# The experts of a mixture-of-experts layer: weight splits traced ahead as one stream, other operations placed behind them

## The chip, the core and the metric

The kernel runs on one core of a Trainium2 chip. The metric is the device time of one execution in microseconds (us). The engines named below are PE (TensorE, matrix products), ACT (ScalarE), DVE (VectorE), POOL (GpSimd) and SP (SyncE, which only issues transfers here).

## The reference, cut to what matters

The layer is a diffusion-transformer block: a gated linear attention and a Hyena convolution, mixed by a projection, then a mixture of experts by expert choice, then a final norm. The change touches only the experts. There are 16 of them; each picks 128 of the 1024 rows.

```
def _ec_moe(h, w_router, w_gate, w_up, w_down):
    cap = EC_FACTOR * L // N_EXPERTS                      # 2 * 1024 // 16 = 128
    aff = jax.nn.softmax((h @ w_router).astype(jnp.float32), axis=-1)
    vals, idx = lax.top_k(jnp.swapaxes(aff, 1, 2), cap)
    xs = h[bidx, idx]
    hid = jax.nn.silu(jnp.einsum('becd,edf->becf', xs, w_gate)) * jnp.einsum('becd,edf->becf', xs, w_up)
    y = jnp.einsum('becf,efd->becd', hid, w_down) * vals[..., None]
    return jnp.zeros_like(h).at[bidx, idx].add(y)
```

All three weight matrices of an expert are 1024x1024 in float32, so the experts read 16 x 3 x 4 MiB.

## The kernel before, in words

A product of float32 accuracy is made of three products: each operand is split into a rounded part `hi` and the remainder `lo`, and `mm3` (lines 150 to 152) adds hi*hi, hi*lo and lo*hi in PSUM. `split` makes the parts: ACT copies the source to `hi` (line 144), DVE subtracts `hi` from the source to get `lo` (line 147).

An expert has three units of products: `w_gate`, `w_up` and `w_down`, called here g, u and d with the expert's number (g3, u3, d3). A unit goes over k = 0 to 7, one weight tile of 128x1024 for each k ("tile k" below). `expert_mm` does it: the tile `raw` is loaded (`expert_tile`; `eraw` for gate and up, `erawl` for down; SP issues the load), split into `ehi` (5 buffers) and `elo` (4 buffers), and multiplied in six matmuls of 512 columns into `pex` (3 buffers in PSUM). So ACT can split a tile only when PE has finished the tile five before it, and DVE only when PE has finished the one four before it. The units come in the order g0, u0, g1, d0, u1, g2, d1, and so on to u15, d15: the gate of the next expert stands between up and down.

Around the units stands other work, each on the in-order queues of its engines:

- `transposed(e, xs, True)` turns the rows of an expert: 8 transposes on PE (`ptx`, line 1341), 8 scalings on ACT (`tt`, line 1346), then a split into `thi` and `tlo` in two halves. Even and odd experts use different `thi` and `tlo`. It is traced in the middle of u(e-1).
- `route(e)` finds an expert's rows: a comparison on DVE (`oh`, line 1320), 8 small matmuls (`pi`), three small DVE operations (`pv`, `ix`, `iv`), and a gather of the rows on POOL (`xs`, one buffer). It is traced in the middle of u(e-2).
- the silu of the gate on ACT (`sg`, line 1354), its product with up on DVE (`sg`, line 1375), and `transposed(e, sg)` of the result, traced in the middle of g(e+1).
- the scaled output `y` on DVE (line 1386), and its scatter-add into DRAM on POOL (`d_acc`, line 1387).

The order of the instructions of one engine is not written out: a scheduler lays them out from the order in which they are traced and from its own estimate of when each can start. `tc.issue_after(x)` keeps each operation of its block, on x's engine, behind x. Behind the experts, eight row tiles `xf` are read back, normed (a square on ACT, an rsqrt of small steps, a scaling on DVE at line 1414) and written, and the last expert's `y` is added to its own rows (lines 1417 to 1425).

Of the kernel before, what the change touches and what calls it, by code (L numbers as in the profile page):

```python
# [10 lines left out]
F32 = mybir.dt.float32  # L11
F32R = mybir.dt.float32r
BF16 = mybir.dt.bfloat16
I32 = mybir.dt.int32
AF = mybir.ActivationFunctionType
# [5 lines left out]
P = 128  # L21
D = 1024
# [4 lines left out]
KT = D // P  # L27
# [5 lines left out]
E = 16  # L33
# [65 lines left out]
def tile_gla_hyena_moe(ctx: ExitStack, tc: tile.TileContext, io: dict, out: bass.AP):  # L99
    nc = tc.nc  # L100
    V, A, T, G, SY = nc.vector, nc.scalar, nc.tensor, nc.gpsimd, nc.sync
# [26 lines left out]
    def pB(shape, name="pb"):  # L128
        return psum.tile(shape, F32, name=name, tag="pB", bufs=2)
# [12 lines left out]
    def split(hi, lo, src, act=True):  # L142
        if act:
            A.activation(hi, src, AF.Copy)  # L144
        else:
            V.tensor_copy(hi, src)
        V.tensor_sub(lo, src, hi.bitcast(F32))  # L147

    def mm3(out_, lh, ll, rh, rl, first, last):
        T.matmul(out_, lh, rh, start=first, stop=False)  # L150
        T.matmul(out_, lh, rl, start=False, stop=False)  # L151
        T.matmul(out_, ll, rh, start=False, stop=last)  # L152
# [40 lines left out]
    def cv(shape, dt=F32, name="cv"):  # L193
        return cp.tile(shape, dt, name=name, tag="cv", bufs=7)
# [24 lines left out]
    for o in range(2):  # L219
        raw = cv([P, 2, HYW], name="w3raw")  # L220
# [19 lines left out]
    for c in range(2):  # L240
        cs = slice(c * 512, (c + 1) * 512)
        ps = pB([P, 512], name="pmlp")
# [8 lines left out]
    for c in range(2):  # L251
        cs = slice(c * 512, (c + 1) * 512)
        ps = pB([P, 512], name="pmlp")
# [268 lines left out]
    ahead = []  # L522
# [393 lines left out]
    def mid_tile(name, dt=F32):  # L916
        return mid.tile([P, D], dt, name=name, tag="x", bufs=NX)
# [18 lines left out]
    state, qe, at = [None] * (2 * NT), [None] * NT, [None] * NT  # L936
# [85 lines left out]
    def row_of(i, pool, **kw):  # L1022
        t = pool.tile([P, D], F32, name=f"row{i}", **kw)
        bcast_row(t, d_mod[0, i * D:(i + 1) * D], D)
        return t
# [175 lines left out]
    pse = ctx.enter_context(tc.tile_pool(name="pse", bufs=1, space=PSUM, reuse_waits="tile"))  # L1201

    def mt(shape, dt, name, tag, bufs):
        return mp.tile(shape, dt, name=name, tag=tag, bufs=bufs)

    def pT(shape, name):
        return pse.tile(shape, F32, name=name, tag="t", bufs=2)

    NR, NL, NHI, NLO, NS, NXS = 14, 8, 5, 4, 4, 1
    used = [0]  # L1210
    KB, KU = 5, 2

    def expert_tile(w, e, k, queue=SY):
        if w == "w_down":
            raw = mt([P, D], F32, "erawl", "erawl", NL)
        else:
            used[0] += 1
            if (used[0] - 1) % (NR + NX) < NX:
                raw = mid_tile("eraw")
            else:  # L1220
                raw = rawr.tile([P, D], F32, name="eraw", tag="eraw", bufs=NR)
        queue.dma_start(raw, io[w][0, e, k * P:(k + 1) * P, :])
        return raw

    loaded = {(w, k): expert_tile(w, 0, k) for w in ("w_gate", "w_up", "w_down") for k in range(KT)}

    def expert_mm(w, e, xt, between=None, at=KB):
        ps = pse.tile([P, D], F32, name="pex", tag="ex", bufs=3)
        for k in range(KT):
            raw = loaded[w, k] if e == 0 else expert_tile(w, e, k)  # L1230
            hi = mt([P, D], F32R, "ehi", "ehi", NHI)
            lo = mt([P, D], F32R, "elo", "elo", NLO)
            split(hi, lo, raw)
            for h in range(2):
                hs = slice(h * 512, (h + 1) * 512)
                mm3(ps[:, hs], xt[0][:, k], xt[1][:, k], hi[:, hs], lo[:, hs], k == 0, k == KT - 1)
            if between and k == at:
                between()
        return ps

    pos = mp.tile([P, E, NT], BF16, name="pos")

# [74 lines left out]
    def route(e):  # L1317
        pi = pT([P, 5], "pi")
        oh = mt([P, NT, P], BF16, "oh", "s2", NS)
        V.tensor_tensor(oh, slot[:, None, :].to_broadcast([P, NT, P]),  # L1320
                        pos[:, e, :, None].to_broadcast([P, NT, P]), op=ALU.is_equal)
        for t in range(NT):
            T.matmul(pi, oh[:, t], tv[:, e, t], start=t == 0, stop=t == NT - 1)
        ix = tiny.tile([P, 1], I32, name="ix", bufs=4)
        pv = tiny.tile([P, 5], F32, name="pv", bufs=4)
        V.tensor_copy(pv, pi)
        last = V.tensor_add(ix, pv[:, 0:1], pv[:, 1:2])
        iv = tiny.tile([P, 1], F32, name="iv", bufs=4)
        V.tensor_reduce(iv, pv[:, 2:5], AX.X, ALU.add)
        xs_ = mt([P, D], F32, "xs", "xs", NXS)  # L1330
        gather = G.indirect_dma_start(out=xs_, out_offset=None, in_=d_h[:, :],
                             in_offset=bass.IndirectOffsetOnAxis(ap=ix[:, :1], axis=0))
        return iv, ix, xs_, last, gather

    def transposed(e, src, norm=False):
        hi = mt([P, KT, P], F32R, "thi", f"thi{e % 2}", 1)
        lo = mt([P, KT, P], F32R, "tlo", f"tlo{e % 2}", 1)
        for g in range(2):
            pt = pT([P, 4, P], "ptx")
            for k in range(4):  # L1340
                T.transpose(pt[:, k], src[:, (4 * g + k) * P:(4 * g + k + 1) * P], ident)  # L1341
            if norm:
                tt = mt([P, 4, P], F32, "tt", "s2", NS)
                for k in range(4):
                    kk_ = 4 * g + k
                    A.activation(tt[:, k], pt[:, k], AF.Identity, bias=fcol[:, 0, kk_:kk_ + 1], scale=gfcol[:, kk_:kk_ + 1])  # L1346
                pt = tt
            split(hi[:, 4 * g:4 * g + 4], lo[:, 4 * g:4 * g + 4], pt)
        return hi, lo

    def gate_part(e, xt, between=None):
        pg = expert_mm("w_gate", e, xt, between)
        sg = mt([P, D], F32, "sg", "sg", 1)
        A.activation(sg, pg, AF.Silu)
        return sg

    A.preload_act_table_set("silu_and_others")
    routed = [route(0)]
    xt = transposed(0, routed[0][2], True)
    routed.append(route(1))  # L1360
    select(NF, E - NF, "b", 2)
    with tc.issue_after(routed[0][3].ins):
        sg = gate_part(0, xt)
    m5 = row_of(5, mp)
    for e in range(E):
        ahead = []

        def next_rows():
            if e + 1 < E:
                ahead.append(transposed(e + 1, routed[e + 1][2], True))  # L1370
            if e + 2 < E:
                routed.append(route(e + 2))

        pu = expert_mm("w_up", e, xt, next_rows, KU)
        V.tensor_mul(sg, pu, sg)
        if e + 1 < E:
            sg_next = gate_part(e + 1, ahead[0], lambda: ahead.append(transposed(e, sg)))
        else:
            ahead = [None, transposed(e, sg)]
        xt_next, ht = ahead  # L1380
        py = expert_mm("w_down", e, ht)
        iv, ix = routed[e][0:2]
        if e + 1 == E:
            break
        y = mt([P, D], F32, "y", "y", 1)
        V.scalar_tensor_tensor(y, py, iv, m5, op0=ALU.mult, op1=ALU.mult)  # L1386
        G.indirect_dma_start(out=d_acc[:, :], out_offset=bass.IndirectOffsetOnAxis(ap=ix[:, :1], axis=0),  # L1387
                             in_=y, in_offset=None, compute_op=ALU.add)
        xt, sg = xt_next, sg_next


    tc.keep_in_program_order(A.preload_act_table_set("natural_log_exp_and_others"))
# [6 lines left out]
    for i in range(NT):  # L1399
        xt = rawr.tile([P, D], F32, name="xf", tag="eraw", bufs=NR)  # L1400
# [45 lines left out]
```

## Time and profile before

| what | value |
|---|---|
| runs | 1383.40, 1385.44, 1390.76 us; median 1385.44 |
| profiled execution, its own time | 1382.24 us |
| its span on the core | 1380.5 us |
| PE busy with matmuls | 1275.1 us (92%) |
| DVE busy | 1149.6 us (83%) |
| ACT busy | 806.4 us (58%) |
| experts' products, first to last start | 769.6 to 1354.3 us |

The span is the stretch in which the profiler saw the core at work; the 1.74 us between it and the execution's time lie around it. Busy times are sums of recorded durations. The record of a matmul reaches past the start of the next one, so a PE that is shown busy throughout can still lose time between two starts; starts are the safer measure.

### The profile page before, as it was taken

To read this page: it belongs to the slowest core of one execution; us is meant where nothing else is said; L and a number is where in the kernel's file an instruction comes from. 1 tells how busy PE (TensorE), PEld (TensorE's weight loads), DVE (VectorE), ACT (ScalarE), POOL (GpSimd) and SP (SyncE) were. 2 spreads that over 40 slices of the span, in tenths; PEclk is the share of its full clock that TensorE was granted. 3 is DMA by queue.
4 is the path that set the end of the run, shared out by engine and by line. 5 is a ranking of instruction groups with operands and counts; after the bars stand their busy time and mean duration, and the time that the engine had idled before them with its cause. 6 is when DMAs were issued, how large, how long until landed. Compare 5 with 4: busy or idle time off the path is not lost.

```text
span 1380.5 us, 21546 instructions
## 1 busy us (share of the span) xinstructions
PE 1275.1 (92%) x7720; PEld 1043.0 (76%) x7720; DVE 1149.6 (83%) x1920; ACT 806.4 (58%) x1228; POOL 130.1 (9%) x142
## 2 busy tenths in 40 slices
PE   6978999999999997987996899999999999999982
PEld 4777888687898896766775678888888888877762
DVE  6877838899778778878756799999999999988885
ACT  3247453211221415885553578888888888877864
POOL 1110000010100110000000000011111111012010
PEclk9998999999999998998996799999999999999996
DMA  7893541774655536766668689999999999999765
GB/s 223 315 241 118 177 128 47 229 218 146 187 169 167 154 100 186 176 158 174 221 230 348 241 316 357 358 394 381 395 381 390 385 389 383 372 366 370 265 204 223
DMA packets 154362, 354.81 MB, mean 257 GB/s; under 512 B 28389, under 2 KB 74013, under 8 KB 153999
## 3 DMA queue, kind: packets, MB, share of 16 engines
q1 hardware_dynamic: 134911, 292.84, 59.7%
q0 software_dynamic: 19344, 60.61, 15.7%
q8 instruction: 60, 0.98, 0.3%
q14 instruction: 47, 0.39, 0.1%
HBM read 310.89 MB, written 50.89 MB: 262 GB/s over the span
## 4 chain that ended last, share of the span: by engine, by line
PE 45%; DVE 4%; DMA 2%; issue 1%; ACT 1%; SPq 0%; POOLq 0%; POOL 0%; DVEq 0%; ACTq 0%
PE pex L151 13%; PE pex L152 12%; PE pex L150 12%; PE ptx L1341 2%; DVE elo L147 1%; PE psel L1252 1%; PE pout L150 1%; DMA eraw<-w_up 1%; PE pout L151 1%; DVE xf L1414 1%; PE pout L152 1%; DVE state L635 0%; PE po L1123 0%; PE po L1127 0%; DMA xs<-d_h,ix 0%
## 5 line engine op out<-in xcount | busy, mean ns | idle before, releaser
L147 DVE TENSOR_TENSOR elo<-eraw,ehi 128x1024 fp32r<-128x1024 f32 x256 | 302.5, 1219 | 13.0 <-issue 5.9
L151 PE MATMUL pex<-elo,thi 128*128 128x512 f32 x768 | 306.0, 398 | 4.7 <-DVE elo L147 4.4
L150 PE MATMUL pex<-ehi,thi 128*128 128x512 f32 x768 | 305.4, 398 | 2.3 <-ACT thi L144 1.3
L152 PE MATMUL pex<-ehi,tlo 128*128 128x512 f32 x768 | 303.4, 395 | 0.8 <-DVE tlo L147 0.8
L144 ACT ACTIVATE ehi<-eraw 128x1024 fp32r<-128x1024 f32 x256 | 265.0, 1068 | 50.2 <-PE pex L152 49.3
L151 PEld LDWEIGHTS pex<-elo,thi 128*128 128x128 f32 x768 | 145.2, 189 | 40.4 <-DVE elo L147 10.4
L150 PEld LDWEIGHTS pex<-ehi,thi 128*128 128x128 f32 x768 | 145.2, 189 | 34.1 <-ACT thi L144 1.7
L152 PEld LDWEIGHTS pex<-ehi,tlo 128*128 128x128 f32 x768 | 145.0, 189 | 31.7 <-DVE tlo L147 1.2
L147 DVE TENSOR_TENSOR elo<-erawl,ehi 128x1024 fp32r<-128x1024 f32 x128 | 149.4, 1218 | 6.4 <-ACT ehi L144 5.6
L144 ACT ACTIVATE ehi<-erawl 128x1024 fp32r<-128x1024 f32 x128 | 131.3, 1057 | 19.6 <-PE pex L152 18.0
L144 ACT ACTIVATE whi<-wraw 128x1024 fp32r<-128x1024 f32 x30 | 31.8, 1060 | 104.9 <-DMA wraw<-w_in 28.4
L542 PE MATMUL phy<-xh,whi 128*128 128x512 f32 x192 | 77.2, 402 | 11.3 <-ACT whi L144 11.3
L543 PE MATMUL phy<-xl,whi 128*128 128x512 f32 x192 | 76.0, 396 | 0.0
L150 PE MATMUL pvg<-whi,xh 128*128 128x256 f32 x256 | 73.2, 286 | 0.0
L151 PE MATMUL pvg<-wlo,xh 128*128 128x256 f32 x256 | 72.4, 283 | 0.0
L152 PE MATMUL pvg<-whi,xl 128*128 128x256 f32 x256 | 72.4, 283 | 0.0
L1387 POOL DMA_INDIRECT d_acc<-y,ix x15 | 34.6, 2308 | 392.5 <-DVE y L1386 392.5
L1346 ACT ACTIVATE tt<-ptx,fcol,gfcol 128x128 f32<-128x128 f32 x128 | 48.7, 463 | 33.9 <-PE ptx L1341 33.9
L545 PE MATMUL phy<-xh,wlo 128*128 128x512 f32 x192 | 61.9, 399 | 0.0
L438 ACT ACTIVATE D<-pdft 128x512 f32<-128x512 f32 x32 | 19.1, 597 | 68.9 <-PE pdft L468 39.4
L147 DVE TENSOR_TENSOR wlo<-wraw,whi 128x1024 fp32r<-128x1024 f32 x30 | 36.6, 1221 | 21.2 <-ACT whi L144 21.1
L467 PE MATMUL pdft<-kk,fmat 128*128 128x128 f32 x256 | 52.1, 286 | 0.3 <-ACT D L438 0.2
(452 smaller groups left out, 2596.3 us busy)
## 6 DMA issues: line engine op xcount, KB each, us to landing
eraw<-w_gate SPq DMA_DIRECT2D x128, 512.0 KB
eraw<-w_up SPq DMA_DIRECT2D x128, 512.0 KB
erawl<-w_down SPq DMA_DIRECT2D x128, 512.0 KB
wt<-w_ada SPq DMA_DIRECT2D x48, 512.0 KB
wraw<-w_in SPq DMA_DIRECT2D x30, 512.0 KB
kspec<-d_spec SPq DMA_DIRECT2D x16, 512.0 KB
xt<-x SPq DMA_DIRECT2D x8, 512.0 KB
d_spec<-ue POOLq DMA_DIRECT2D x8, 512.0 KB, 5.9
```

The source lines that it names most:

```text
L144: A.activation(hi, src, AF.Copy)
L147: V.tensor_sub(lo, src, hi.bitcast(F32))
L150: T.matmul(out_, lh, rh, start=first, stop=False)
L151: T.matmul(out_, lh, rl, start=False, stop=False)
L152: T.matmul(out_, ll, rh, start=False, stop=last)
L467: T.matmul(ps[:, r], fmat[:, r, m1], kk[m1 // 4][:, 0, m1 % 4], start=True, stop=False)
L542: T.matmul(ps[:, h], hi[:, k], rh[k][:, h], start=k == 0, stop=False)
L543: T.matmul(ps[:, h], hi[:, k], rl[k][:, h], start=False, stop=False)
L545: T.matmul(ps[:, h], lo[:, k], rh[k][:, h], start=False, stop=k == KT - 1)
L1341: T.transpose(pt[:, k], src[:, (4 * g + k) * P:(4 * g + k + 1) * P], ident)
L1346: A.activation(tt[:, k], pt[:, k], AF.Identity, bias=fcol[:, 0, kk_:kk_ + 1], scale=gfcol[:, kk_:kk_ + 1])
L1387: G.indirect_dma_start(out=d_acc[:, :], out_offset=bass.IndirectOffsetOnAxis(ap=ix[:, :1], axis=0), in_=y, in_offset=None, compute_op=ALU.add)
```

## The change

The 48 units are written out as a list, and their 384 weight tiles as one stream. `split_ahead(t)`, called ahead of the products of tile t, traces the ACT copies up to tile t+4 and the DVE subtractions up to tile t+3, across the units' borders. Everything else (rows, route, hidden, silu, the product with up, y) is traced in a block that keeps it behind the last copy and the last subtraction traced by then, but for the last expert's transposes. The places move as well: the next rows from u tile 2 to u tile 3, the transposes of the hidden rows from g tile 5 to g tile 2, and `route`, which was traced with the rows in u, to g tile 5. `m5` (a row that `y` needs) is traced ahead of the first unit now. No operation is added or left out, and no shape changes.

```
--- before.py
+++ after.py
@@ -1208,7 +1208,6 @@
 
     NR, NL, NHI, NLO, NS, NXS = 14, 8, 5, 4, 4, 1
     used = [0]
-    KB, KU = 5, 2
 
     def expert_tile(w, e, k, queue=SY):
         if w == "w_down":
@@ -1223,20 +1222,6 @@
         return raw
 
     loaded = {(w, k): expert_tile(w, 0, k) for w in ("w_gate", "w_up", "w_down") for k in range(KT)}
-
-    def expert_mm(w, e, xt, between=None, at=KB):
-        ps = pse.tile([P, D], F32, name="pex", tag="ex", bufs=3)
-        for k in range(KT):
-            raw = loaded[w, k] if e == 0 else expert_tile(w, e, k)
-            hi = mt([P, D], F32R, "ehi", "ehi", NHI)
-            lo = mt([P, D], F32R, "elo", "elo", NLO)
-            split(hi, lo, raw)
-            for h in range(2):
-                hs = slice(h * 512, (h + 1) * 512)
-                mm3(ps[:, hs], xt[0][:, k], xt[1][:, k], hi[:, hs], lo[:, hs], k == 0, k == KT - 1)
-            if between and k == at:
-                between()
-        return ps
 
     pos = mp.tile([P, E, NT], BF16, name="pos")
 
@@ -1348,45 +1333,96 @@
             split(hi[:, 4 * g:4 * g + 4], lo[:, 4 * g:4 * g + 4], pt)
         return hi, lo
 
-    def gate_part(e, xt, between=None):
-        pg = expert_mm("w_gate", e, xt, between)
-        sg = mt([P, D], F32, "sg", "sg", 1)
-        A.activation(sg, pg, AF.Silu)
-        return sg
+
+
+    units = [("w_gate", 0)]
+    for e in range(E):
+        units += [("w_up", e)] + ([("w_gate", e + 1)] if e + 1 < E else []) + [("w_down", e)]
+    stream = [(w, e, k) for w, e in units for k in range(KT)]
+    AH, AL = NHI - 1, NLO - 1
+    his, los, last_split = [], [], [None, None]
+
+    def split_ahead(t):
+        while len(his) <= min(t + AH, len(stream) - 1):
+            w, e, k = stream[len(his)]
+            raw = loaded[w, k] if e == 0 else expert_tile(w, e, k)
+            hi = mt([P, D], F32R, "ehi", "ehi", NHI)
+            last_split[0] = A.activation(hi, raw, AF.Copy)
+            his.append((hi, raw))
+        while len(los) <= min(t + AL, len(stream) - 1):
+            hi, raw = his[len(los)]
+            lo = mt([P, D], F32R, "elo", "elo", NLO)
+            last_split[1] = V.tensor_sub(lo, raw, hi.bitcast(F32))
+            los.append(lo)
+
+    def behind_splits():
+        stack = ExitStack()
+        for x in last_split:
+            stack.enter_context(tc.issue_after(x.ins))
+        return stack
+
+    def unit(j, xt, hooks):
+        ps = pse.tile([P, D], F32, name="pex", tag="ex", bufs=3)
+        for k in range(KT):
+            t = KT * j + k
+            split_ahead(t)
+            for h in range(2):
+                hs = slice(h * 512, (h + 1) * 512)
+                mm3(ps[:, hs], xt[0][:, k], xt[1][:, k], his[t][0][:, hs], los[t][:, hs], k == 0, k == KT - 1)
+            if k in hooks:
+                with behind_splits():
+                    hooks[k]()
+        return ps
 
     A.preload_act_table_set("silu_and_others")
     routed = [route(0)]
-    xt = transposed(0, routed[0][2], True)
+    rows_t = {0: transposed(0, routed[0][2], True)}
     routed.append(route(1))
     select(NF, E - NF, "b", 2)
-    with tc.issue_after(routed[0][3].ins):
-        sg = gate_part(0, xt)
     m5 = row_of(5, mp)
-    for e in range(E):
-        ahead = []
-
-        def next_rows():
-            if e + 1 < E:
-                ahead.append(transposed(e + 1, routed[e + 1][2], True))
-            if e + 2 < E:
-                routed.append(route(e + 2))
-
-        pu = expert_mm("w_up", e, xt, next_rows, KU)
-        V.tensor_mul(sg, pu, sg)
-        if e + 1 < E:
-            sg_next = gate_part(e + 1, ahead[0], lambda: ahead.append(transposed(e, sg)))
-        else:
-            ahead = [None, transposed(e, sg)]
-        xt_next, ht = ahead
-        py = expert_mm("w_down", e, ht)
+    sgs, hts = {}, {}
+
+    def rows_ahead(e):
+        rows_t[e] = transposed(e, routed[e][2], True)
+
+    def gated(e, pg):
+        sgs[e] = mt([P, D], F32, "sg", "sg", 1)
+        A.activation(sgs[e], pg, AF.Silu)
+
+    def add_rows(e, py):
         iv, ix = routed[e][0:2]
-        if e + 1 == E:
-            break
         y = mt([P, D], F32, "y", "y", 1)
         V.scalar_tensor_tensor(y, py, iv, m5, op0=ALU.mult, op1=ALU.mult)
         G.indirect_dma_start(out=d_acc[:, :], out_offset=bass.IndirectOffsetOnAxis(ap=ix[:, :1], axis=0),
                              in_=y, in_offset=None, compute_op=ALU.add)
-        xt, sg = xt_next, sg_next
+
+    def hidden(e):
+        hts[e] = transposed(e, sgs.pop(e))
+
+    for j, (w, e) in enumerate(units):
+        hooks = {}
+        if w == "w_up" and e + 1 < E:
+            hooks[3] = lambda: rows_ahead(e + 1)
+        elif w == "w_gate" and e > 0:
+            hooks[2] = lambda: hidden(e - 1)
+            if e + 1 < E:
+                hooks[5] = lambda: routed.append(route(e + 1))
+        if w == "w_down" and e + 1 == E:
+            hidden(e)
+        if j == 0:
+            with tc.issue_after(routed[0][3].ins):
+                ps = unit(j, rows_t[0], hooks)
+        else:
+            ps = unit(j, hts.pop(e) if w == "w_down" else rows_t[e], hooks)
+        with behind_splits():
+            if w == "w_gate":
+                gated(e, ps)
+            elif w == "w_up":
+                V.tensor_mul(sgs[e], ps, sgs[e])
+            elif e + 1 < E:
+                add_rows(e, ps)
+    py = ps
+    iv, ix = routed[E - 1][0:2]
 
 
     tc.keep_in_program_order(A.preload_act_table_set("natural_log_exp_and_others"))
```

**Place 1.** DVE, the end of expert 11's down unit and the up unit of expert 12 (`erawl` are tiles of d11, `eraw` those of u12 and then g13). Before:

```order
L147 TENSOR_TENSOR elo<-erawl,ehi 128x1024 x8
L147 TENSOR_TENSOR elo<-eraw,ehi 128x1024
L1386 SCALAR_TENSOR_TENSOR y<-pex,iv,row_7853 128x1024
L147 TENSOR_TENSOR elo<-eraw,ehi 128x1024 x2
L1320 TENSOR_TENSOR oh<-slot,pos 128x1024
L147 TENSOR_TENSOR tlo<-tt,thi 128x512
L1326 COPY pv<-pi 128x5
L1327 TENSOR_TENSOR ix<-pv 128x1
L1329 TENSOR_REDUCE iv<-pv 128x1
L147 TENSOR_TENSOR elo<-eraw,ehi 128x1024
L147 TENSOR_TENSOR tlo<-tt,thi 128x512
L147 TENSOR_TENSOR elo<-eraw,ehi 128x1024 x6
```

The same place of the change:

```order
L1355 TENSOR_TENSOR elo<-erawl,ehi 128x1024 x5
L1355 TENSOR_TENSOR elo<-eraw,ehi 128x1024 x3
L1395 SCALAR_TENSOR_TENSOR y<-pex,iv,row_7770 128x1024
L1355 TENSOR_TENSOR elo<-eraw,ehi 128x1024 x5
L147 TENSOR_TENSOR tlo<-tt,thi 128x512
L1355 TENSOR_TENSOR elo<-eraw,ehi 128x1024
L147 TENSOR_TENSOR tlo<-tt,thi 128x512
L1355 TENSOR_TENSOR elo<-eraw,ehi 128x1024 x2
L1421 TENSOR_TENSOR sg<-pex,sg 128x1024
```

`y` stood behind one subtraction of the new unit here, as it does for experts 12 to 14, and stands behind three now; in the kernel before it stood behind four for experts 1 to 9 and three for expert 10, in the change behind three for every expert. The `oh` of route has left the up unit.

**Place 2.** DVE, from the border of up and gate to the down unit, experts 5 to 6 (it repeats in the change up to u10). Before, from the last tiles of u5 through g6 into d5:

```order
L147 TENSOR_TENSOR elo<-eraw,ehi 128x1024
L1375 TENSOR_TENSOR sg<-pex,sg 128x1024
L147 TENSOR_TENSOR elo<-eraw,ehi 128x1024 x6
L147 TENSOR_TENSOR elo<-erawl,ehi 128x1024 x2
L147 TENSOR_TENSOR tlo<-ptx,thi 128x512 x2
L147 TENSOR_TENSOR elo<-erawl,ehi 128x1024 x6
```

The same place of the change:

```order
L1355 TENSOR_TENSOR elo<-eraw,ehi 128x1024
L147 TENSOR_TENSOR tlo<-tt,thi 128x512
L1355 TENSOR_TENSOR elo<-eraw,ehi 128x1024
L1421 TENSOR_TENSOR sg<-pex,sg 128x1024
L1355 TENSOR_TENSOR elo<-eraw,ehi 128x1024 x3
L147 TENSOR_TENSOR tlo<-ptx,thi 128x512 x2
L1355 TENSOR_TENSOR elo<-eraw,ehi 128x1024 x2
L1355 TENSOR_TENSOR elo<-erawl,ehi 128x1024
L1305 TENSOR_TENSOR oh<-slot,pos 128x1024
L1355 TENSOR_TENSOR elo<-erawl,ehi 128x1024
L1311 COPY pv<-pi 128x5
L1355 TENSOR_TENSOR elo<-erawl,ehi 128x1024
```

The second half of the rows' `tlo` now follows the subtraction of g tile 1, the hidden rows' `tlo` come within the gate unit, and `oh` with what follows it stands in the down unit, between tiles 0 and 2. On PE the 8 `pi` matmuls now stand behind the third matmul of d tile 0.

**Place 3.** DVE, behind the last subtraction of the last unit. Before:

```order
L1417 SCALAR_TENSOR_TENSOR y<-pex,iv,row_7853 128x1024
L156 TENSOR_SCALAR rs_x<-fms 128x2
L1418 TENSOR_TENSOR y<-y,rows 128x1024
L161 TENSOR_TENSOR rs_t<-rs_y 128x2
L162 TENSOR_TENSOR rs_t<-rs_t,rs_x 128x2
L163 TENSOR_SCALAR rs_t<-rs_t 128x2
L164 TENSOR_TENSOR frs<-rs_y,rs_t 128x2
L1414 SCALAR_TENSOR_TENSOR xf<-xf,frs,gfin 128x1024 x2
```

Of the change:

```order
L156 TENSOR_SCALAR rs_x<-fms 128x2
L161 TENSOR_TENSOR rs_t<-rs_y 128x2
L162 TENSOR_TENSOR rs_t<-rs_t,rs_x 128x2
L163 TENSOR_SCALAR rs_t<-rs_t 128x2
L164 TENSOR_TENSOR frs<-rs_y,rs_t 128x2
L1450 SCALAR_TENSOR_TENSOR xf<-xf,frs,gfin 128x1024 x2
L156 TENSOR_SCALAR rs_x<-fms 128x2
L1453 SCALAR_TENSOR_TENSOR y<-pex,iv,row_7770 128x1024
```

The first pair of normed tiles stands ahead of the last expert's `y` instead of behind it.

## Rows read from the trace of the kernel before

**Rows 1.** Busy time by stretch: length, PE, PEld, DVE, ACT, POOL, clock, DMA, GB/s.

```profile
800.00:824.00 24.00, 23.50 (x125) 18.39 (x124) 23.51 (x30) 17.71 (x19) 0.95 (x1) 1.00 0.87 321
...
972.00:1009.00 37.00, 36.98 (x177) 30.22 (x176) 35.70 (x36) 32.09 (x43) 3.69 (x2) 1.00 1.03 393
...
1194.00:1231.00 37.00, 35.24 (x157) 28.08 (x156) 32.41 (x33) 28.51 (x36) 4.22 (x2) 0.95 1.00 373
```

**Rows 2.** Timeline of POOL, scatter-adds of experts 1, 9, 11 and 14: start, duration.

```profile
862.02 2.31 POOL L1387 DMA_INDIRECT d_acc<-y,ix  x1 [23.32 <-DVE y L1386]
...
1144.37 2.31 POOL L1387 DMA_INDIRECT d_acc<-y,ix  x1 [26.17 <-DVE y L1386]
...
1213.99 2.31 POOL L1387 DMA_INDIRECT d_acc<-y,ix  x1 [26.93 <-DVE y L1386]
...
1329.29 2.29 POOL L1387 DMA_INDIRECT d_acc<-y,ix  x1 [34.88 <-DVE y L1386]
```

**Rows 3.** Timeline of DVE, start of u12; in brackets idle before, and releaser.

```profile
1209.18 1.22 DVE L147 TENSOR_TENSOR elo<-eraw,ehi 128x1024 fp32r<-128x1024 f32 x1
1212.42 1.28 DVE L1386 SCALAR_TENSOR_TENSOR y<-pex,iv,row 128x1024 f32<-128x1024 f32 x1 [2.02 <-PE pex L152]
1213.62 2.35 DVE L147 TENSOR_TENSOR elo<-eraw,ehi 128x1024 fp32r<-128x1024 f32 x2
```

**Rows 4.** Timeline of PE, tile 3 of u12.

```profile
1218.90 0.49 PE L150 MATMUL pex<-ehi,thi 128*128 128x512 f32 x1 [0.98 <-ACT ehi L144]
1220.16 0.63 PE L151 MATMUL pex<-elo,thi 128*128 128x512 f32 x1 [0.77 <-DVE elo L147]
```

**Rows 5.** The tile eraw: idle time of engines until its loads landed (us, times).

```profile
  DMA eraw<-w_gate: 0.6, 1
```

**Rows 6.** Timeline of PE, u15 tile 1 and d15 tile 0.

```profile
1330.20 0.50 PE L151 MATMUL pex<-elo,thi 128*128 128x512 f32 x1 [0.89 <-DVE elo L147]
...
1343.97 0.50 PE L152 MATMUL pex<-ehi,tlo 128*128 128x512 f32 x1 [0.79 <-DVE tlo L147]
```

**Rows 7.** Timeline of PE: transposes in g6, first matmuls of d5, u6, d6 and u7.

```profile
985.97 1.03 PE L1341 MATMUL ptx<-ident,sg 128*128 128x128 f32 x8
986.76 0.48 PE L150 MATMUL pex<-ehi,thi 128*128 128x512 f32 x1
...
989.62 0.39 PE L150 MATMUL pex<-ehi,thi 128*128 128x512 f32 x1
...
1000.50 0.40 PE L150 MATMUL pex<-ehi,thi 128*128 128x512 f32 x1
...
1024.74 0.40 PE L150 MATMUL pex<-ehi,thi 128*128 128x512 f32 x1
...
1035.89 0.39 PE L150 MATMUL pex<-ehi,thi 128*128 128x512 f32 x1
```

**Rows 8.** Timeline of DVE in g6 and d5, and y of expert 5.

```profile
978.97 6.89 DVE L147 TENSOR_TENSOR elo<-eraw,ehi 128x1024 fp32r<-128x1024 f32 x6
985.78 2.35 DVE L147 TENSOR_TENSOR elo<-erawl,ehi 128x1024 fp32r<-128x1024 f32 x2
988.05 1.28 DVE L147 TENSOR_TENSOR tlo<-ptx,thi 128x512 fp32r<-128x512 f32 x2
...
1001.67 1.28 DVE L1386 SCALAR_TENSOR_TENSOR y<-pex,iv,row 128x1024 f32<-128x1024 f32 x1
```

**Rows 9.** Timeline of ACT in u5, around the next rows.

```profile
970.58 1.83 ACT L1346 ACTIVATE tt<-ptx,fcol,gfcol 128x128 f32<-128x128 f32 x5
...
973.84 1.09 ACT L144 ACTIVATE ehi<-eraw 128x1024 fp32r<-128x1024 f32 x1
```

**Rows 10.** The tile xs: its 16 gathers, from issue to landing.

```profile
DMA to landing us min/median/max: 4.6/7.8/12.2
```

**Rows 11.** Timeline of DVE behind the last product.

```profile
1354.76 1.28 DVE L1417 SCALAR_TENSOR_TENSOR y<-pex,iv,row 128x1024 f32<-128x1024 f32 x1 [4.39 <-PE pex L152]
...
1358.00 2.48 DVE L1414 SCALAR_TENSOR_TENSOR xf<-xf,frs,gfin 128x1024 f32<-128x1024 f32 x2
```

## The prediction

> **What bounds the kernel now.** I read the busy time by stretch first, to see which part of the experts runs at its limit. In the middle PE is busy 36.98 of 37 us at full clock, with DVE at 35.70; in the stretch from 1194 us PE falls to 35.24 and its clock to 0.95 [rows 1]. So the middle is at PE's limit and the end isn't.
>
> The scatter-adds of POOL then give the period of an expert, since one follows each down unit. From expert 1 to expert 9 eight periods take 1144.37 - 862.02 = 282.35 us, 35.29 each. Experts 12 to 14 take 1329.29 - 1213.99 = 115.30 us, where three such periods are 105.88: 9.4 us are lost there [rows 2]. No operation differs between these experts, so the loss must come from order or from data.
>
> The timelines show it to be order. At u12 DVE made one subtraction, then reached `y` and stood 2.02 us, because `y` waits for the whole of d11. The subtractions of u12's tiles 1 and 2 stood behind it and began only at 1213.62, when PE was already in the new unit [rows 3]. ACT had the same trouble: the scalings of the next rows stood ahead of the copy of tile 3, and PE waited 0.98 us for that copy, then 0.77 for its subtraction. The matmul behind that is recorded with 0.63 us against 0.39 in a run without waits: the granted clock of this stretch is 0.95 in the mean, so part of it ran at 1.2 GHz and not at 2.4 [rows 1, 4, 7]. Data is not the reason, since engines waited for a tile of `eraw` 0.6 us in all, once [rows 5]. At the end of the experts the same shape returns: 0.89 us at u15 tile 1, behind `y` of expert 14, and 0.79 at d15 tile 0, where the low part of the hidden rows stands behind two subtractions [rows 6].
>
> **The change part by part.** Nothing is added or removed, so each edit is worth what it does to a queue.
>
> *`y` and the copies, experts 12 to 14.* In the change `y` has three subtractions ahead of it. It takes some 1.2 us and the next subtraction 1.14 (6.81 us between the first of six and what follows it [rows 8]), 2.3 together, while PE has three tiles of 6 x 0.227 = 1.36 us each (d5 takes 10.88 us for 48 matmuls, 0.227 apart [rows 7]), 4.1 us. So `y` hides, as it did behind four in the middle: there it ran at 1001.67 without idle time ahead of it [rows 8]. The copies of the rest of u and of g tile 0 stand ahead of the next rows. I take these experts to the period of the middle: -9.4 us. Bounds: 0 if something else holds them, and about -10 if the small stalls around u11 go as well.
>
> *The end of the experts.* At u15 `y` is behind three subtractions, and at d15 one instead of two stands ahead of the low part. The idle times are 0.89 and 0.79, and PE lost more than it was idle: a matmul is recorded for 0.39 us where the next starts after 0.227, so 0.16 of each pause is covered by a record [rows 6, 7]. Together 2.0 us: -2.0, bounds -1 and -2.3.
>
> *The tail.* In the kernel before DVE stood 4.39 us ahead of the last `y`, and the first pair of normed tiles began 3.24 us after that `y` began, since it was behind it [rows 11]. Now the pair is ahead of `y`. DVE can use part of that pause, but ACT's squares must be ready and they wait for ACT to finish its copies. What follows, six scalings and the last `y`, is unchanged. I take half of the 3.24 us: -1.5, bounds 0 and -3.2.
>
> *The middle.* Here the change can only cost. Let T be the time when PE ends u tile 3 and starts the transposes of the next rows. These hold PE 0.79 us [rows 7]. ACT is free to begin the copy of g tile 0 at T + 0.2 (its buffer is freed by u tile 3); behind it come five scalings, a half of `thi` and three scalings, which take 973.84 - 970.58 = 3.26 us [rows 9]. With 1.0 for the copy ahead of them, the copy of g tile 1 starts at T + 4.4 and ends, after 1.09, at T + 5.5. DVE waits for it, and then has in order: g1, a `tlo`, g2, the product with up, g3, g4, g5, two `tlo`, g6. That is seven long operations of 1.135 us and three halves of 0.6 (two are recorded with 1.28 together), 9.75 us [rows 8]: g tile 6 is split at T + 15.3. PE needs it one matmul into that tile: 0.8 + 4 tiles + 6 tiles + the hidden rows' transposes 0.8 + 0.2 = T + 15.4 at 1.36 a tile, T + 15.6 at the 1.38 that two slower and two faster experts average. After three more long operations `oh` ends at T + 18.7. PE wants it behind half of d tile 0: T + 18.6 to 18.9. So the margin is between -0.1 and +0.3 us at two places of each expert, and from there on DVE gains 0.2 us on every tile. I charge 0.05 us for each of 13 experts, +0.6; bounds 0 and 0.5 each, 6.5, the second if my margins are half a microsecond too kind, since a DVE that is late there is late for every expert.
>
> All of this takes PE's spacing from the row: the 48 matmuls of d5 start 227 ns apart with no wait among them [rows 7]. The Trainium skill, page TensorE: Matmul & The Clock Gate, section Back-to-back issue gap, gives some 131 ns for sustained matmuls of 512 columns. The trace disagrees, and the measurement decides. By the Trainium skill's figure PE would have slack all through the middle and DVE would pace it, which is the fifth rival; by the row the middle has nothing to give.
>
> *The gather.* `route` now comes within the period before its rows are used; it came a whole period earlier. `ix` comes at about T + 21.5 and the rows are transposed at T + 35.3, a period after T. The gather has 13.8 us from there. The longest of 16 landings took 12.2 us, the median 7.8 [rows 10]. I take it as hidden; if the landing grows, the first to wait is PE at `ptx`, and the copies behind `tt` on ACT.
>
> *The start.* In u0, g1 and d0 the select of the other experts' rows shares DVE and PE. PE is busy 23.50 of 24 us there with DVE at 23.51 [rows 1]. Little is to be won, and two subtractions now stand ahead of the next rows: 0, bounds -0.5 and +1.5.
>
> Sum: -9.4 - 2.0 - 1.5 + 0.6 = -12.3 us. The profiled execution took 1382.24 us (1380.5 of span and 1.74 around it), so its like would take 1369.9. It was 3.2 us (0.23%) under the median of the runs, 1385.44, and I apply the difference to the median: 1373.1.
>
> **The rivals.**
>
> 1. *DVE paces the middle.* For it: DVE is busy 35.70 of 37 us in the middle and will spend most of the 1.3 to 1.8 us that it has left of a period waiting for the copy of g tile 1; my margins are worked out to 0.1 us and the waits between engines are not. Against it: if PE is late, all that is counted from T is late with it, and DVE's own work in a period is 24 x 1.135 = 27.2 for the subtractions, 2.4 for four halves, some 3.5 for the three operations of like size and 0.4 of small ones, 33.5 us [rows 8]; by its busy share, 35.70 of 37, it is 34.0 at most. At 0.5 to 1 us for each of 13 experts the gain shrinks by 6.5 to 13: 1379 to 1386. From 1.5 us on it ends on the slow side.
>
> 2. *Gathers come late (slower).* From a landing of about 13.8 us on, PE waits at `ptx` in every one of 14 experts. At 16.4 us, with weights and the rest at 393 GB/s beside it [rows 1], 2.6 us each are 36 us: 1409. Against it: the gather leaves some 25 us after the scatter-add of the expert before, so its own queue is empty, and the longest landing is short of the point.
>
> 3. *The late stalls have another cause.* Then only the end and the tail give: 1385.4 - 3.5 + 0.6 = 1382.5. Against it: the waits name `y` and the copies.
>
> 4. *The buffers' places.* d5, of an odd expert, takes 10.88 us for its 48 matmuls, d6 1035.89 - 1024.74 = 11.15, without waits [rows 7]; the other units alternate in the same way. I don't know which operand's place sets this, and `m5` now comes ahead of `ehi` and `elo`. 24 units at 0.27 are 6.5 us: 1366.6 if all become fast, 1379.6 if all become slow.
>
> 5. *Matmuls closer than 0.227 us.* If splits further ahead let PE start them closer, DVE's 33.5 us is the period: 14 times 1.8 us, 25 us less: 1348. Against it: in d5 both parts were there in time, and the spacing was still 0.227.
>
> **How the numbers follow.** Forecast 0.72; rival 1 0.14; rival 2 0.04; rival 3 0.04; rival 4 0.05, even on both sides; rival 5 0.01. What a measurement of this kernel can tell from no change is about 0.5%, 6.9 us: faster means under 1378.5, slower over 1392.4. The forecast, rival 5 and half of rival 4 are faster, 0.76; rival 2 and the far end of rival 1 are slower, 0.05; the rest, 0.19, lies within. The low end of the range, 1367, is the forecast with the tail's full bound and the stalls of u11 and some spread of runs; the high end, 1382, takes in the slow side of rival 4, most of rival 3 and the milder half of rival 1.
>
> **What would show it.** Right: scatter-adds of POOL 35.3 us apart up to expert 14; no wait of PE over 0.3 us in u12 to u15 tile 1; granted clock 1.00 from 1194 us on; the first `xf` scaling ahead of the last `y`. Wrong: a wait of PE for `oh` or for `elo` at g tile 6 or d tile 0 in each expert (rival 1); PE waiting for `xs` at `ptx` (rival 2); the same losses after expert 11 (rival 3); even and odd units equally long (rival 4). The prediction would fail most easily by the margin of `oh`: each 0.5 us there costs half the gain.

## The result

The changed kernel takes 1409.44 us (median of 4 runs, 1404.65 to 1413.22), the kernel before 1386.46 on the same chip (4 runs, 1383.40 to 1390.76): a ratio of 1.0156, interval 1.0120 to 1.0192. It is slower, and the forecast of 1373, range 1367 to 1382, is missed on the far side. The profiled execution took 1404.65 us, 1402.9 of them span, 22.4 more than before.

The list of PE's waits begins with a row whose like was 5.6 us, one wait, in the kernel before; the columns are the total, the number of waits and the longest. Under it the tile `xs` of the same kernel: the shortest, median and longest gather instruction on POOL in ns, and the time from issue to landing. The landings stand against [rows 10].

```profile
PE ptx L1326 <- DMA xs<-d_h,ix: 28.8, 8, 6.0
```

```profile
L1316 POOL DMA_INDIRECT xs<-d_h,ix x16: 1264/1374/9267, 762.8 to 1303.8; - x16
...
DMA to landing us min/median/max: 4.7/8.4/16.6
```

The rows that PE transposes are late, and the gather that fetches them is long before its transfer begins: 9.3 us on POOL where the median is 1.4. The timeline of POOL shows that it is every second one, and that the scatter-add behind it is long too:

```profile
890.71 1.31 POOL L1316 DMA_INDIRECT xs<-d_h,ix  x1 [21.04 <-PE pex L151]
900.70 2.32 POOL L1396 DMA_INDIRECT d_acc<-y,ix  x1 [8.68 <-DVE y L1395]
926.35 9.26 POOL L1316 DMA_INDIRECT xs<-d_h,ix  x1 [23.34 <-PE pex L152]
936.23 6.84 POOL L1396 DMA_INDIRECT d_acc<-y,ix  x1 [0.62 <-DVE y L1395]
```

What DVE did around 926 us, and what PE did behind the late gather (in brackets: idle before, and what ended it):

```profile
925.46 0.15 DVE L1312 TENSOR_TENSOR ix<-pv 128x1 int32<-128x1 f32 x1
925.53 0.15 DVE L1314 TENSOR_REDUCE iv<-pv 128x1 f32<-128x3 f32 x1
925.60 5.75 DVE L1355 TENSOR_TENSOR elo<-erawl,ehi 128x1024 fp32r<-128x1024 f32 x5
931.27 3.49 DVE L1355 TENSOR_TENSOR elo<-eraw,ehi 128x1024 fp32r<-128x1024 f32 x3
934.68 1.27 DVE L1395 SCALAR_TENSOR_TENSOR y<-pex,iv,row 128x1024 f32<-128x1024 f32 x1
```

```profile
942.81 1.70 PE L1326 MATMUL ptx<-ident,xs 128*128 128x128 f32 x8 [3.01 <-DMA xs<-d_h,ix]
...
944.74 0.63 PE L151 MATMUL pex<-elo,thi 128*128 128x512 f32 x1
945.16 0.63 PE L152 MATMUL pex<-ehi,tlo 128*128 128x512 f32 x1
```

The gather ends at 926.35 + 9.26 = 935.61, 0.93 us after `y` has begun, and `y` is the first operation of DVE behind a run of eight weight subtractions. The scatter-add behind it stands again under a run of subtractions. After the 3.01 us pause PE also starts its matmuls 0.42 us apart instead of 0.227 [rows 7]. The busy time by stretch, columns as in [rows 1], has the granted clock (third number from the end) at 0.59 over these 4.2 us, most of them at the lower of its two levels, 1.2 GHz, and at 1.00 behind them. The 4.2 us are worth 4.2 x 0.41 = 1.7 us less than at the full clock.

```profile
942.80:947.00 4.20, 4.19 (x16) 3.62 (x17) 0.28 (x1) 3.30 (x10) 0.28 (x1) 0.59 1.06 393
947.00:962.00 15.00, 15.00 (x71) 12.39 (x70) 14.19 (x15) 12.39 (x15) 0.00 (x0) 1.00 0.93 346
```

To see where the time went, stage by stage, I take marks that all kernels have: the silu of a gate unit, which ACT starts when PE ends it, and PE's last product. First the kernel before (gates 0, 1, 11 and 15, and the last product), then the changed one:

```profile
785.23 1.03 ACT L1354 ACTIVATE sg<-pex 128x1024 f32<-128x1024 f32 x1
812.76 1.03 ACT L1354 ACTIVATE sg<-pex 128x1024 f32<-128x1024 f32 x1 [0.32 <-PE pex L152]
1166.14 1.03 ACT L1354 ACTIVATE sg<-pex 128x1024 f32<-128x1024 f32 x1 [0.30 <-PE pex L152]
1316.00 1.03 ACT L1354 ACTIVATE sg<-pex 128x1024 f32<-128x1024 f32 x1 [2.72 <-PE pex L152]
1354.33 0.39 PE L152 MATMUL pex<-ehi,tlo 128*128 128x512 f32 x1
```

```profile
787.50 1.02 ACT L1390 ACTIVATE sg<-pex 128x1024 f32<-128x1024 f32 x1
814.42 1.03 ACT L1390 ACTIVATE sg<-pex 128x1024 f32<-128x1024 f32 x1 [0.25 <-PE pex L152]
...
887.66 1.03 ACT L1390 ACTIVATE sg<-pex 128x1024 f32<-128x1024 f32 x1 [0.26 <-PE pex L152]
923.04 1.03 ACT L1390 ACTIVATE sg<-pex 128x1024 f32<-128x1024 f32 x1 [0.29 <-PE pex L152]
962.94 1.03 ACT L1390 ACTIVATE sg<-pex 128x1024 f32<-128x1024 f32 x1 [0.25 <-PE pex L152]
...
1187.43 1.03 ACT L1390 ACTIVATE sg<-pex 128x1024 f32<-128x1024 f32 x1 [0.26 <-PE pex L152]
1342.64 1.03 ACT L1390 ACTIVATE sg<-pex 128x1024 f32<-128x1024 f32 x1 [0.25 <-PE pex L152]
1378.17 0.39 PE L152 MATMUL pex<-ehi,tlo 128*128 128x512 f32 x1
```

From 887.66 to 923.04 a period takes 35.38 us, from 923.04 to 962.94, with the late gather in it, 39.90. Gates 1 to 11 took 353.38 us before and take 373.01. From gate 15 on the changed kernel is ahead: 35.53 us to the last product against 38.33.

### The profile page after: what moved, and what is told of

Same layout as the page of the kernel before. It is cut to its first block, busy times and chain, and to the rows that moved or that the text cites. A ratio compares the mean times of both kernels' runs of the same rounds, so it can differ in the third digit from the quotient of the medians.

```text
span 1402.9 us, 21543 instructions
## 1 busy us (share of the span) xinstructions
PE 1280.1 (91%) x7720; PEld 1049.5 (75%) x7720; DVE 1145.3 (82%) x1920; ACT 812.4 (58%) x1228; POOL 218.6 (16%) x142
## 4 chain that ended last, share of the span: by engine, by line
PE 28%; issue 12%; DMA 10%; DVE 3%; ACT 1%; SPq 0%; POOLq 0%; DVEq 0%; POOL 0%
DMA xs<-d_h,ix 8%; PE pex L150 7%; PE pex L151 7%; PE pex L152 7%; PE ptx L1326 2%; PE psel L1237 1%; PE pout L150 1%; PE pout L151 1%; DMA eraw<-w_up 1%; PE pout L152 1%; DVE xf L1450 1%; DVE state L635 0%; PE po L1123 0%; PE po L1127 0%; PE pth L1166 0%
## 5 line engine op out<-in xcount | busy, mean ns | idle before, releaser
L150 PE MATMUL pex<-ehi,thi 128*128 128x512 f32 x768 | 308.9, 403 | 1.3 <-ACT thi L144 1.3
L1316 POOL DMA_INDIRECT xs<-d_h,ix x16 | 76.7, 4794 | 367.0 <-PE pex L152 180.1
L1396 POOL DMA_INDIRECT d_acc<-y,ix x15 | 73.2, 4883 | 100.6 <-DVE y L1395 100.6
```

## The experiments

My theory: POOL's gather is held while DVE runs a row of subtractions with both inputs in SBUF, and `route` now comes right ahead of such a row. The Trainium skill, page SBUF — State Buffer, sections SBUF: two separate sides and Who interferes with whom, says that a DVE instruction with two SBUF inputs contends with a GpSimd instruction that reads SBUF, and that the loser is blocked for the whole instruction. The second of these sections also reports a probe in which `tensor_tensor`, the operation of the subtractions here, did not stall a DMA; if the subtractions hold the gather, the 9.26 us above differ from that and decide. The rivals: transfers beside the gather make it slow (the second rival of the forecast), or the new order of splits is slow by itself (the first).

**Route where it was.** The changed kernel, with `route` traced with the next rows again.

```
         if w == "w_up" and e + 1 < E:
-            hooks[3] = lambda: rows_ahead(e + 1)
+            def rows_and_route():
+                rows_ahead(e + 1)
+                if e + 2 < E:
+                    routed.append(route(e + 2))
+            hooks[3] = rows_and_route
...
-                hooks[5] = lambda: routed.append(route(e + 1))
```

> The changed kernel with one thing undone: route is traced with the next rows in u, behind u tile 3, as in the kernel before, not in g behind tile 5. The stream of splits and all else stay. Late rows (whatever makes them late): the gather has a whole period more, no wait of PE at ptx for xs is left, the pairs of experts no longer alternate by 4 to 7 us, and the time falls by about 35 us to 1369 to 1375, at my first forecast. Rival, the new order of splits is what costs: the time stays at 1400 to 1412 and u tile 3 still takes over 5 us.

Measured: 1376.83 us (6 runs, 1374.41 to 1383.89), ratio to before 0.9927 (0.9899 to 0.9954). The longest gather is 1.43 us on POOL, the longest landing 9.2 us, and PE's only wait for `xs` is the first expert's, 5.8 us. The new order of splits is not what costs; late rows are. The time is some 2 us above what I expected.

**A small operation in the run.** Two kernels add a copy of 128x5 on DVE, two subtractions behind `iv`; one reads `pi` in PSUM, the other `pv` in SBUF. A third, run once, has a subtraction `pv - pv` there, with two SBUF inputs.

```
+        elif w == "w_down" and e + 2 < E:
+            hooks[1] = lambda: V.tensor_copy(tiny.tile([P, 5], F32, name="brk", bufs=4), routed[e + 2][5])
```

> The changed kernel with one tiny VectorE operation added: a second copy of pi (128x5, read from PSUM) that comes two weight subtractions behind iv, so in the middle of the run of 8 subtractions up to y. Theory (GpSimd's gather is held while VectorE runs subtractions with both inputs in SBUF, until one that reads PSUM): every gather instruction ends within about 2.5 us instead of 9.3 us in every second expert, the longest landing falls from 16.6 to about 10 us, PE waits no more at ptx, and the time is 1369 to 1378. Rival, transfers beside the gather or the queue are what is slow: the landings stay at up to 16 us and the time at 1400 to 1412.

> As the run with the copy from PSUM, at the same place and of the same size, but the tiny copy reads pv in SBUF. If GpSimd gets its turn only at an instruction that reads PSUM: the 9.3 us gathers stay, and the time is 1400 to 1412, as without it. If any instruction with fewer than two SBUF inputs, or any break in the run, is enough: as with the copy from PSUM, 1369 to 1378.

> As the run with the small copy of pv, but the small operation is a subtraction with two inputs in SBUF (pv minus pv, 128x5). If the two SBUF inputs of the large subtractions are what holds GpSimd, this one does not let it in: gathers of 9.3 us in every second expert and a span of about 1400. If any small instruction that breaks the run of equal large ones lets it in: all gathers at about 2.5 us, span about 1369.

Measured: with the copy from PSUM 1372.49 us (4 runs), ratio 0.9890 (0.9864 to 0.9915); with the copy from SBUF 1370.64 us (4 runs, 1370.36 to 1372.32), ratio 0.9877 (0.9852 to 0.9903); with the subtraction a span of 1370.2 us. In all three every gather from d1 on takes 2.44 to 2.47 us. Timelines of DVE and of POOL with the copy from SBUF:

```profile
887.34 0.15 DVE L1314 TENSOR_REDUCE iv<-pv 128x1 f32<-128x3 f32 x1
887.41 2.35 DVE L1355 TENSOR_TENSOR elo<-erawl,ehi 128x1024 fp32r<-128x1024 f32 x2
889.68 0.17 DVE L1411 COPY brk<-pv 128x5 f32<-128x5 f32 x1
```

```profile
888.17 2.45 POOL L1316 DMA_INDIRECT xs<-d_h,ix  x1 [18.36 <-PE pex L152]
898.12 6.86 POOL L1396 DMA_INDIRECT d_acc<-y,ix  x1 [7.50 <-DVE y L1395]
```

The gather ends at 890.62, 0.94 us after the copy has begun; in the changed kernel it was 0.93 us after `y`. One operation of 0.17 us, which has nothing to do with the gather's data, shortens it from 9.26 to 2.45 us, and 38.8 us of the time go with it (1409.44 - 1370.64). So DVE's order holds the gather, and the weights' transfers, which are the same, don't. That the release needs an instruction that reads PSUM, or one with fewer than two SBUF inputs, is refuted: the two-input subtraction released it as well. The scatter-add, which nobody waits for, still stands 6.86 us.

**Route late, in the kernel before.**

```
-            if e + 2 < E:
-                routed.append(route(e + 2))
+        def hidden_and_route():
+            ahead.append(transposed(e, sg))
+            if e + 2 < E:
+                routed.append(route(e + 2))
...
-            sg_next = gate_part(e + 1, ahead[0], lambda: ahead.append(transposed(e, sg)))
+            sg_next = gate_part(e + 1, ahead[0], hidden_and_route)
```

> The kernel before with one part of the change alone: route is traced behind g tile 5 (with the transposes of the hidden rows) instead of in u with the next rows. The splits stay as they were. Theory (route's place is what costs): the index now comes ahead of a run of 9 or 10 subtractions up to y here too, gathers of about 9 us appear, PE waits at ptx in u, and the time rises by 20 to 40 us from 1386 to 1406 to 1426. Rival, the cost needs the new order of splits: it stays within 1380 to 1392.

Measured: 1392.85 us (10 runs), ratio 1.0035 (1.0017 to 1.0053). My theory gave 20 us or more, so here it failed by most of its size. In the profiled execution, at 1399.33 us the longest of the ten, one gather, in d0, was held for 12.64 us, with the longest landing, 19.9; the thirteen behind it took 1.30 to 1.32 us, although seven to nine subtractions stood between `iv` and `y` there too. How long a hold lasts follows the run of subtractions; whether there is a hold at all does not.

**Route three tiles earlier.** In the changed kernel, behind g tile 2, with no copy (`hooks[2]`: `hidden(e - 1)`, then `route(e + 1)`).

> The changed kernel with route three tiles earlier, in g behind tile 2 with the hidden rows, and no small copy. The index then comes some 4 us earlier, still ahead of a run of subtractions (11 of them, up to y). Theory: a gather that is held waits until y here too, over 10 us, so it ends no earlier than in the changed kernel, and what counts is whether it gets its turn ahead of the run; with holds in every second expert 1395 to 1412, with none 1368 to 1374. Rival, only the distance between route and the rows counts: 4 us more are enough, no PE wait at ptx, 1368 to 1374 with holds of about 9 us or more.

Measured: 1402.94 us, ratio 1.0103 (1.0076 to 1.0130). The row of subtractions is longer, and so is the hold, again in every second expert:

```profile
892.01 1.31 POOL L1316 DMA_INDIRECT xs<-d_h,ix  x1 [17.16 <-PE pex L152]
...
927.73 12.66 POOL L1316 DMA_INDIRECT xs<-d_h,ix  x1 [19.92 <-PE pex L152]
```

A head start of 4 us was eaten by 3.4 us more of holding. Distance alone does not help as long as `y` is what ends the hold.

**Why every second expert?** One kernel, run once, was meant to swap the places of the two sets of `thi` and `tlo`, since the products of odd experts take 1.36 us a tile and those of even ones 1.40 (an unused pair of tiles is put ahead, and `tlo` is changed like `thi`).

```
+    mt([P, KT, P], F32R, "thi", "thi0", 1), mt([P, KT, P], F32R, "tlo", "tlo0", 1)
...
-        hi = mt([P, KT, P], F32R, "thi", f"thi{e % 2}", 1)
+        hi = mt([P, KT, P], F32R, "thi", f"thi{(e + 1) % 2}", 1)
```

> The changed kernel with the two sets of buffers for transposed rows (thi and tlo) swapped between even and odd experts, nothing else. In the changed kernel the gathers traced in the faster d units (1.36 us a tile, odd experts) are held and those in the slower ones (1.40) are not. If it is the pace of the products that decides, the held gathers move to the other experts: u3, u5, u7 take 15 to 18 us and u4, u6, u8 about 12, span about 1400. If it is something else that goes by turns: the late units stay u2, u4, u6.

Measured: span 1409.8 us. It did not do what I meant: all units took 1.40 us a tile. But the holds still alternated, in the same experts, with no difference of pace left to follow. The next kernel gives the small copy only to the experts whose gathers were held.

```
-        elif w == "w_down" and e + 2 < E:
+        elif w == "w_down" and e + 2 < E and e % 2 == 1:
```

> The changed kernel with the small copy of pv only in the d units of odd experts (d1, d3 to d13), whose gathers were held for 9.3 us; the gathers of d2, d4 to d12, which passed in 1.3 us, are left as they were. If being held is tied to an expert (its buffers, its addresses), those stay short, no rows are late, and the time is 1369 to 1374 as with copies in all. Rival, they passed only because PE had stalled just before and VectorE had caught up: with the stalls gone they are held in their turn, u3, u5, u7 take 15 to 17 us and u2, u4, u6 about 12, and the time is 1390 to 1410.

Measured: 1400.56 us, ratio 1.0097 (1.0066 to 1.0128). The holds have moved to the experts that were free of them:

```profile
856.20 2.45 POOL L1316 DMA_INDIRECT xs<-d_h,ix  x1 [18.17 <-PE pex L152]
...
891.36 9.25 POOL L1316 DMA_INDIRECT xs<-d_h,ix  x1 [18.35 <-PE pex L152]
930.83 1.31 POOL L1316 DMA_INDIRECT xs<-d_h,ix  x1 [22.74 <-PE pex L152]
966.36 9.26 POOL L1316 DMA_INDIRECT xs<-d_h,ix  x1 [18.72 <-PE pex L152]
```

So no expert has the hold for itself. In this kernel and in the changed one, from d1 on, a gather with no stall of PE before it is held, and behind a stall the next one passes. What differs between them shows on DVE, at `pv`: its copy of PE's result `pi`, from which `ix` is made. In the changed kernel, ahead of the gather that passed and of the one that was held:

```profile
888.57 0.17 DVE L1311 COPY pv<-pi 128x5 f32<-128x5 f32 x1
888.68 1.23 DVE L1355 TENSOR_TENSOR elo<-erawl,ehi 128x1024 fp32r<-128x1024 f32 x1
...
924.26 0.16 DVE L1311 COPY pv<-pi 128x5 f32<-128x5 f32 x1
924.33 1.21 DVE L1355 TENSOR_TENSOR elo<-erawl,ehi 128x1024 fp32r<-128x1024 f32 x1
```

From the start of `pv` to the next subtraction it is 0.11 us in the first case and 0.07 in the second. I read the longer step as the trace of a DVE that had caught up with PE and waited for `pi`; after a stall DVE is nearer to PE. The sign holds nearly everywhere. Take the gathers of all runs from d0 on that have two or more subtractions without a pause behind `iv`: the 79 that were held have 71 to 73 ns there, and of the 44 that passed 43 have 79 to 431 ns. The exception is the gather at 892.01 of the kernel with route three tiles earlier, with 73. The sign covers route late in the kernel before too: 73 ns in d0, 79 to 110 behind it. In the changed kernel the scatter-adds go the same way: 2.3 us where DVE had paused ahead of `y`, 5.7 to 6.9 us where it had not. This is a sign, not a cause that was shown, since no run changed that pause alone. The time since the silu is no such sign: the held gather began 926.35 - 923.04 = 3.31 us after the silu of its gate, and a later one of the same kernel passed at 1268.17 - 1264.66 = 3.51.

**The half that holds everything behind the splits.** The kernel with the SBUF copy, with `behind_splits()` returning an empty stack.

> The kernel with the small copy of pv (1370.6 us) without the second half of the change: the splits are still traced as one stream ahead of the products, but rows, route, hidden rows, silu, the product with up and y are no longer held behind the last copy and the last subtraction. If holding them back is what takes the late stalls of experts 12 to 14 away, as my forecast has it, u12 to d14 take about 115 us again as in the kernel before, not 107, and the time is 1376 to 1384. Rival, the stream alone does it: 1368 to 1374, and u12 to d14 stay at about 107.

Measured: 1385.48 us (10 runs), ratio 0.9989 (0.9973 to 1.0006): all the gain is gone. Ahead of `y` of experts 12 to 14 there is one subtraction of the new unit again. PE's timeline has the late waits back, of the kind of [rows 4] and [rows 6], and the marks (gates 11 and 15, last product) are 150.32 and 38.34 us apart, as in the kernel before (149.86 and 38.33):

```profile
1222.97 0.50 PE L151 MATMUL pex<-elo,thi 128*128 128x512 f32 x1 [0.60 <-DVE elo L1355]
...
1254.29 0.50 PE L151 MATMUL pex<-elo,thi 128*128 128x512 f32 x1 [0.66 <-DVE elo L1355]
```

```profile
1166.52 1.03 ACT L1387 ACTIVATE sg<-pex 128x1024 f32<-128x1024 f32 x1 [0.28 <-PE pex L152]
1316.84 1.03 ACT L1387 ACTIVATE sg<-pex 128x1024 f32<-128x1024 f32 x1 [2.74 <-PE pex L152]
```

```profile
1355.18 0.39 PE L152 MATMUL pex<-ehi,tlo 128*128 128x512 f32 x1
```

The agreement is of the sums: 1.5 us of the late stretch are two waits of PE for `xs` here, which the kernel before did not have.

## Why the prediction was wrong

The failed step is the gather: "The gather has 13.8 us from there. The longest of 16 landings took 12.2 us, the median 7.8 [rows 10]. I take it as hidden". I read the landing as a property of the transfer. It has two parts, the time for which POOL stands in the instruction and the transfer behind it, and the change altered the first. The room was about right: PE came for the rows at 942.81 - 3.01 = 939.80, 13.45 us after the held gather had begun. The landing was wrong, 16.6 us at the most against 12.2.

The 12.2 us that I used as an upper bound already had a hold in it, and I did not ask why. In the kernel before the gather that landed after 12.2 us stood 5.87 us on POOL, under five subtractions, and ended 0.94 us after the product with up (`sg`) had begun. The row of `xs` in that kernel, and POOL and DVE around that gather:

```profile
L1331 POOL DMA_INDIRECT xs<-d_h,ix x16: 950/1366/5865, 760.9 to 1261.2; - x16
...
1261.24 5.87 POOL L1331 DMA_INDIRECT xs<-d_h,ix  x1 [5.16 <-issue]
...
1260.49 5.75 DVE L147 TENSOR_TENSOR elo<-eraw,ehi 128x1024 fp32r<-128x1024 f32 x5
1266.17 1.22 DVE L1375 TENSOR_TENSOR sg<-pex,sg 128x1024 f32<-128x1024 f32 x1
```

The kernel with the SBUF copy is the change without this error. Its marks, in the same order:

```profile
787.59 1.03 ACT L1390 ACTIVATE sg<-pex 128x1024 f32<-128x1024 f32 x1
814.48 1.03 ACT L1390 ACTIVATE sg<-pex 128x1024 f32<-128x1024 f32 x1 [0.25 <-PE pex L152]
1166.09 1.03 ACT L1390 ACTIVATE sg<-pex 128x1024 f32<-128x1024 f32 x1 [0.25 <-PE pex L152]
1308.73 1.03 ACT L1390 ACTIVATE sg<-pex 128x1024 f32<-128x1024 f32 x1 [0.27 <-PE pex L152]
1344.25 0.39 PE L152 MATMUL pex<-ehi,tlo 128*128 128x512 f32 x1
```

| stretch | before | changed | with copy | with copy against before | forecast |
|---|---|---|---|---|---|
| to the silu of gate 0 | 785.23 | 787.50 | 787.59 | +2.36 | - |
| gate 0 to 1 | 27.53 | 26.92 | 26.89 | -0.64 | 0 (start) |
| gate 1 to 11 | 353.38 | 373.01 | 351.61 | -1.77 | +0.6 (middle) |
| gate 11 to 15 | 149.86 | 155.21 | 142.64 | -7.22 | -9.4 (late stalls) |
| gate 15 to last product | 38.33 | 35.53 | 35.52 | -2.81 | -2.0 (end) |
| last product to the end | 26.17 | 24.73 | 24.65 | -1.52 | -1.5 (tail) |

- *The gather*, taken at 0: 373.01 - 351.61 = 21.40 and 155.21 - 142.64 = 12.57 us, 34.0 together. PE's waits for `xs` behind the first expert are 28.8 - 6.0 = 22.8 of it, in seven experts (the first one, 6.0 us, is there with the copies too, 5.7). For the other 11.2 the lower clock behind the pauses is enough: 1.7 us at the one pause shown, 11.9 for seven like it. The granted clock over the whole span says the same, 0.958 against 0.966 with the copies: 1402.9 x 0.042 - 1368.9 x 0.034 = 12.4 us.
- *Late stalls and end*, -11.4 together, measured -10.0. That the order behind the splits is what takes them away is shown: without it the two stretches are back to within 0.5 us. The first term was 2.2 us too large: the four periods of that stretch take 142.64 / 4 = 35.66 us, not the 35.29 that I gave them, which is 1.5 us of it. The second was 0.8 too small.
- *Tail*, -1.5, measured -1.52: the pair of scalings stands ahead of the last `y`, at 1344.63 and 1347.10 us, the reverse of [rows 11]. The direction was reasoned; that half of the 3.24 us would come was a guess that fell right.
- *Middle*, charged +0.6, gave -1.77. The thin margins did not cost, and that the change "can only cost" here was wrong. Most of the gain goes with the new place of `route`: with route where it was, gates 1 to 11 take 1169.86 - 816.77 = 353.09 us, only 0.29 less than before.
- The 2.36 us ahead of gate 0 I take for spread: that mark lies between 785.2 and 794.0 us in the profiled executions of these kernels, all alike up to the experts.

Of the rivals, the second came nearest: it named the wait at `ptx`, gave 1409 at a landing of 16.4 us, and 16.6 and 1409.4 were measured. That agreement is partly luck. It had the weights' transfers as the cause, which the small copy refutes, and 2.6 us in each of 14 experts, where it is some 5 us in every second one. I gave it 0.04, since I looked only at POOL's own queue. The fifth (matmuls closer than 0.227) did not appear, and by the fourth the units of odd and even experts kept their 1.36 and 1.40 us a tile.

The version to keep is the changed kernel with the small copy from SBUF: 1370.64 us, better than both.

What stays open: why a gather passes between two subtractions when DVE had waited at `pv`, some two microseconds earlier. Held or not, it begins 0.75 us after the start of a subtraction (890.71 against 889.96, and 926.35 against 925.60), and the subtractions follow without a pause.

## What to carry to other kernels

Before you move a gather or scatter that GpSimd issues, look at what VectorE runs from that moment on: behind a row of large operations with two SBUF inputs the instruction may stand until the row is broken, here whenever VectorE came to the row without having waited, with one exception. Read the longest instruction on the issuing engine, not only the landing: if it is several times the median, the tail of the landings may be made by the neighbour's order and move with it, as it did here. Where a hidden transfer has only a microsecond or two to spare, put a small operation in the row, or keep the distance of a whole period.

## What the runs showed of the hardware

- A gather on GpSimd was held for as long as VectorE ran subtractions without a pause: 2.45 us with two behind `iv`, 3.59 with three (in the kernel with nothing held behind the splits), 5.87 with five, 9.26 with eight and 12.66 with eleven. It ended 0.81 to 0.96 us after the next operation of another kind had begun. The Trainium skill, in the sections named above, has the block last for one instruction; here it outlasted up to eleven of 1.13 us each, and that the row acts as one was measured, not explained.
- Each of three small operations ended it: a copy from PSUM, a copy from SBUF, a subtraction with two SBUF inputs, each of 128x5 (2.44 to 2.47 us).
- Whether a gather was held went with DVE's step at `pv`: 71 to 73 ns at all 79 that were held, 79 ns or more at 43 of the 44 that passed. Behind a stall of PE the next gather passed, so the loss shows in every second expert and looks like a matter of buffers.
- A pause of PE of 3.01 us was followed by a granted clock of 0.59 over the next 4.2 us.
